# Loading the last y tile of a batched matmul with one DMA of 24 KB runs instead of four of 6 KB runs

## Chip, cores, metric

One core of one Trainium2 chip. The metric is the device time of one execution in microseconds (us). The profiler's span of the same execution is about 1.8 us shorter, and times inside a trace count from the span's start. All runs quoted here are single-core.

## The reference

```python
x: (32, 256, 512) float32      y: (32, 512, 384) float32
out = np.einsum('bij,bjk->bik', x, y).astype(np.float32)      # (32, 256, 384)
```

That is 16.8 MB of x, 25.2 MB of y and 12.6 MB of output.

## The kernel before

The 32 batches go in eight groups of four (n = 0 to 7). For each group x is loaded, rounded to fp16 and transposed on DVE (VectorE); y is loaded and rounded to fp16 on DVE in four casts, each of a quarter of the tile; TensorE multiplies in two halves (e = 0, 1) of 64 matmuls; ACT (ScalarE) and partly DVE copy PSUM to SBUF; the result is stored. All DMAs are issued by SP (SyncE) and so pass through one queue. In the plan below a line is a stage, and each engine keeps the order in which its own parts stand there: x, y and S are a load or a store, T the transposes, R the casts of y, M the matmuls, C the copies on ACT, D those on DVE.

```python
PLAN = """
x0 x1 y0
T0 x2 y1
T1 R0 M0 C0 x3 y2
... (cut)
T5 D3 R4 M4 C4 x7 y6 S2
T6 D4 R5 M5 C5 y7
T7 D5 R6 M6 C6 R7 M7 C7 D7 S3 S4 S5 S6 S7
"""
... (cut: x and y tiles have 2 buffers each, PSUM all 8 banks)
    def load_y(n):
        y_of[n] = y_pool.tile([P, T, K], F32, name="y_sb")       # 128 x 16 x 384 = 24 KB per partition
        src = y[n * Q : (n + 1) * Q].rearrange("g (q t) k -> (g q) t k", t=T)
        step = STEP if n == N - 1 else T                         # STEP = 4: the last y in four pieces
        for a in range(0, T, step):
            keep(nc.sync.dma_start(out=y_of[n][:, a : a + step], in_=src[:, a : a + step]))
...
    def round_y(n):
        y_sb = y_of.pop(n)
        yr_of[n] = yr_pool.tile([P, T, K], MM_DT, name="y_r")
        for a in range(0, T, STEP):                              # four casts
            keep(nc.vector.tensor_copy(yr_of[n][:, a : a + STEP], y_sb[:, a : a + STEP]))
```

In `multiply` the loop over t runs from 0 to 15 with four matmuls each, so the first quarter of a half needs only the first cast of y. Groups 6 and 7 are stored by two DMAs each (S6a, S6b, S7a, S7b), the others by one.

Of the kernel before, what the change touches and what calls it, by code (L numbers as in the profile page):

```python
# [1 line left out]

# [4 lines left out]


MM_DT = mybir.dt.float16
F32 = mybir.dt.float32  # L10
P = 128


Q = 4
STEP = 4
O_BUFS = 5
WIDE_GROUPS = 6
# [8 lines that stand above are left out]
T2 D0 R1 M1 C1 x4 y3 S0  # L26
T3 D1 R2 M2 C2 x5 y4 S1
T4 D2 R3 M3 C3 x6 y5
# [6 lines that stand above are left out]
@with_exitstack  # L35
def kernel(
    ctx: ExitStack,
    tc: tile.TileContext,
    x: bass.AP,
    y: bass.AP,  # L40
    out: bass.AP,
):
    nc = tc.nc

    B, I, J = x.shape
    _, _, K = y.shape

    PQ = P // Q
    R = I // PQ
    T = J // PQ  # L50
    TW = T // 2
    NE = I // P
    N = B // Q

    x_pool = ctx.enter_context(tc.tile_pool(name="x_pool", bufs=2))
    y_pool = ctx.enter_context(tc.tile_pool(name="y_pool", bufs=2))
    xr_pool = ctx.enter_context(tc.tile_pool(name="xr_pool", bufs=1))
    xt_pool = ctx.enter_context(tc.tile_pool(name="xt_pool", bufs=3))
    yr_pool = ctx.enter_context(tc.tile_pool(name="yr_pool", bufs=2))
    o_pool = ctx.enter_context(tc.tile_pool(name="o_pool", bufs=O_BUFS))  # L60
    psum_pool = ctx.enter_context(
        tc.tile_pool(name="psum", bufs=2 * Q, space=bass.MemoryType.PSUM)
    )

    keep = tc.keep_in_program_order




    x_of, y_of, xt_of, yr_of, ps_of, o_of = {}, {}, {}, {}, {}, {}  # L70

    def width(n):
        return PQ if n < WIDE_GROUPS else 2 * PQ

    def on_vector(n, e, g):
        if n < WIDE_GROUPS:
            return (e, g) == (NE - 1, Q - 1)
        return n == N - 1 and g % 2 == 1

    def load_x(n):  # L80
        x_of[n] = x_pool.tile([P, R, J], F32, name="x_sb")
        keep(
            nc.sync.dma_start(  # L83
                out=x_of[n],
                in_=x[n * Q : (n + 1) * Q].rearrange("g (p r) j -> (g p) r j", r=R),
            )
        )

    def load_y(n):
        y_of[n] = y_pool.tile([P, T, K], F32, name="y_sb")  # L90
        src = y[n * Q : (n + 1) * Q].rearrange("g (q t) k -> (g q) t k", t=T)
        step = STEP if n == N - 1 else T
        for a in range(0, T, step):
            keep(nc.sync.dma_start(out=y_of[n][:, a : a + step], in_=src[:, a : a + step]))

    def transpose_x(n):


        x_r = xr_pool.tile([P, R, J], MM_DT, name="x_r")
        keep(nc.vector.tensor_copy(x_r, x_of.pop(n)))  # L100
        xt_of[n] = xt_pool.tile([P, NE, TW, P], F32, name="xt_sb")
        b = width(n) // PQ
        src = x_r.bitcast(F32).rearrange("p (b h e) (q t) -> p b e t h q", b=b, e=NE, t=TW)
        dst = xt_of[n].rearrange("p e t (h s b) -> p b e t h s", s=PQ, b=b)
        for e in range(NE):
            for c in range(b):
                keep(nc.vector.transpose(dst[:, c, e], src[:, c, e]))  # L107
# [4 lines that stand above are left out]
        for a in range(0, T, STEP):  # L112
            keep(nc.vector.tensor_copy(yr_of[n][:, a : a + STEP], y_sb[:, a : a + STEP]))  # L113

    def multiply(n):
        xt = xt_of.pop(n).bitcast(MM_DT).rearrange("p e t (m c) -> p e t m c", c=2)
        y_r = yr_of.pop(n)
        o_of[n] = o_pool.tile([P, R, K], F32, name="o_sb")
        for e in range(NE):
            for g in range(Q):  # L120
                ps_of[n, e, g] = psum_pool.tile([P, K], F32, name="o_ps")
            for t in range(T):
                for g in range(Q):
                    s = slice(g * PQ, (g + 1) * PQ)
                    keep(
                        nc.tensor.matmul(  # L126
                            ps_of[n, e, g],
                            xt[s, e, t // 2, :, t % 2],
                            y_r[s, t],
                            start=(t == 0),  # L130
                            stop=(t == T - 1),
                        )
                    )

    def collect(n, vector):
        w = width(n)
        per = P // w
        copy = nc.vector.tensor_copy if vector else nc.scalar.copy
        o = o_of[n].rearrange("p (u f) k -> p u f k", u=Q // per)
        for e in range(NE):  # L140
            for g in range(Q):
                if on_vector(n, e, g) != vector:
                    continue
                ps = ps_of.pop((n, e, g))
                a = g % per * w
                for h in range(per):
                    keep(copy(o[a : a + w, g // per, h * NE + e], ps[h * w : (h + 1) * w]))  # L147

    def store(n):
        w = width(n)  # L150
        per = P // w
        o = o_of.pop(n).rearrange("p (u f) k -> p u f k", u=Q // per)
        for u in range(Q // per):
            b = n * Q + u * per
            keep(
                nc.sync.dma_start(  # L156
                    out=out[b : b + per].rearrange("g (s f) k -> (g s) f k", s=w),
                    in_=o[:, u],
                )
            )  # L160

    parts = {
        "x": load_x,
        "y": load_y,
        "T": transpose_x,
        "R": round_y,
        "M": multiply,
        "C": lambda n: collect(n, False),
        "D": lambda n: collect(n, True),
        "S": store,  # L170
    }
    for step in PLAN.split():
        parts[step[0]](int(step[1:]))


# [1 line left out]
_INS = ['x', 'y']  # L177
_OUTS = [((32, 256, 384), 'float32')]


# [23 lines left out]
```

## Time and profile before

| | before |
|---|---|
| time, median of the first 3 runs | 135.26 us (134.78 to 135.62) |
| span of the profiled run | 133.3 us |
| bytes moved, mean rate | 54.68 MB, 410 GB/s |
| DMA packets | 4187 |

The rows by engine of the page have one digit per fortieth of the span, 9 being full. The prediction below shows the lines.

### The profile page before, as it was taken

The page shows a single profiled execution, that of the slowest core. Times are in us where ns is not written, and L with a number is a line of the kernel's source. Part 1 is how long each engine was busy: PE and PEld are TensorE (multiplying, and loading weights), DVE is VectorE, ACT ScalarE, POOL GpSimd, SP SyncE. Part 2 cuts the span into 40 slices and gives each one's busy share as a digit, 9 for nine tenths or more (in the row PEclk, how much of TensorE's full clock was granted, in tenths as well). Part 3 has the DMA queues.
Part 4 walks back from the last instruction along what each step waited for, and adds up shares of the span by engine and source line. Part 5 has one row for each costly group of instructions (what it writes and reads, how often), then busy time and mean ns, then how long its engine had stood idle before and what let it go on. Part 6 is the DMA issues. An engine that isn't in the chain of part 4 may idle for free.

```text
span 133.3 us, 2449 instructions
## 1 busy us (share of the span) xinstructions
PE 58.7 (44%) x1024; PEld 35.6 (27%) x1024; DVE 96.3 (72%) x92; ACT 91.5 (69%) x193; POOL 0.2 (0%) x4
## 2 busy tenths in 40 slices
PE   0000004960398039806980079200991398776000
PEld 0000002530255025503450046000560275444000
DVE  0049999699969999999069990999999965255300
ACT  3000000099999999999999997999459999997200
POOL 0000000000000000000000000000000000000000
PEclk9999999998569855995599559955599558999655
DMA  5999999999999999999999999999999999999992
GB/s 103 428 423 438 457 413 423 465 406 423 418 472 428 393 433 430 406 400 449 435 457 392 436 423 452 433 401 452 428 428 389 419 424 443 408 432 425 408 415 107
DMA packets 4187, 54.68 MB, mean 410 GB/s; under 512 B 464, under 2 KB 464, under 8 KB 1488
## 3 DMA queue, kind: packets, MB, share of 16 engines
q1 hardware_dynamic: 4176, 54.53, 97.0%
q8 instruction: 8, 0.13, 0.4%
q14 instruction: 3, 0.02, 0.0%
HBM read 41.94 MB, written 12.58 MB: 409 GB/s over the span
## 4 chain that ended last, share of the span: by engine, by line
DMA 39%; DVE 21%; PE 16%; ACT 15%; issue 1%; DVEq 0%; SPq 0%
DMA x_sb<-in_x_dram 39%; PE o_ps L126 16%; ACT o_sb L147 15%; DVE xt_sb L107 7%; DVE o_sb L147 6%; DVE x_r L100 5%; DVE y_r L113 2%; DVEq L199 0%; SPq L156 0%; DVEq L100 0%; SPq L83 0%
## 5 line engine op out<-in xcount | busy, mean ns | idle before, releaser
L147 ACT COPY o_sb<-o_ps 32x384 f32<-32x384 f32 (+1 forms) x192 | 90.2, 470 | 31.8 <-PE o_ps L126 25.9
L126 PE MATMUL o_ps<-y_r,xt_sb 32*128 32x384 f16 x1024 | 58.7, 389 | 63.5 <-DVE y_r L113 60.7
L126 PEld LDWEIGHTS <-xt_sb 32*128 32x128 f16 x1024 | 35.6, 110 | 86.2 <-issue 54.3
L100 DVE CAST x_r<-x_sb 128x4096 f16<-128x4096 f32 x8 | 18.4, 2294 | 19.0 <-DMA x_sb<-in_x_dram 18.9
L107 DVE STREAM_TRANSPOSE xt_sb<-x_r 128x1024 f32<-128x1024 f32 (+1 forms) x20 | 31.6, 1629 | 0.3
L113 DVE CAST y_r<-y_sb 128x1536 f16<-128x1536 f32 x32 | 28.8, 953 | 3.4 <-DMA y_sb<-in_y_dram 3.2
L147 DVE COPY o_sb<-o_ps 32x384 f32<-32x384 f32 (+1 forms) x32 | 17.8, 556 | 5.4 <-PE o_ps L126 4.9
L147 ACT ACT_TABLE_LOAD x1 | 1.3, 1283 | 0.7 <-PEq L188 0.7
L188 POOL MEMSET const-bfloat16-1.0<- 128x1 bf16 x1 | 0.1, 101 | 0.0
L188 POOL MEMSET const-uint8-127<- 128x1 uint8 x1 | 0.1, 101 | 0.0
L188 POOL MEMSET const-float32-0.0<- 128x1 f32 x1 | 0.1, 98 | 0.2 <-issue 0.2
L188 POOL MEMSET const-float32-1.0<- 128x1 f32 x1 | 0.1, 98 | 0.0
## 6 DMA issues: line engine op xcount, KB each, us to landing
y_sb<-in_y_dram SPq DMA_DIRECT2D x7, 3072.0 KB, 22.9
x_sb<-in_x_dram SPq DMA_DIRECT2D x8, 2048.0 KB, 22.5
out_dram<-o_sb SPq DMA_DIRECT2D x6, 1536.0 KB, 23.0
y_sb<-in_y_dram SPq DMA_DIRECT2D x4, 768.0 KB, 14.8
out_dram<-o_sb SPq DMA_DIRECT2D x4, 768.0 KB, 8.5
```

Of the source, the lines that this page charges most:

```text
L100: keep(nc.vector.tensor_copy(x_r, x_of.pop(n)))
L107: keep(nc.vector.transpose(dst[:, c, e], src[:, c, e]))
L113: keep(nc.vector.tensor_copy(yr_of[n][:, a : a + STEP], y_sb[:, a : a + STEP]))
L126: nc.tensor.matmul(ps_of[n, e, g], xt[s, e, t // 2, :, t % 2], y_r[s, t], start=(t == 0), stop=(t == T - 1),)
L147: keep(copy(o[a : a + w, g // per, h * NE + e], ps[h * w : (h + 1) * w]))
L188: nc = _bacc.Bacc("TRN2", target_bir_lowering=False, num_devices=1)
```

## The change

The last y is treated like the other seven: one DMA whose 128 runs are 24 KB long, in place of four with 128 runs of 6 KB each. A run with a size is a stretch of contiguous bytes in one partition; the page counts a packet for each, and one more for each engine's report that a DMA has ended. The intent is fewer descriptors, completions and issues. What is given up: the first cast could start when a quarter of the tile was there.

```diff
     def load_y(n):
         y_of[n] = y_pool.tile([P, T, K], F32, name="y_sb")
-        src = y[n * Q : (n + 1) * Q].rearrange("g (q t) k -> (g q) t k", t=T)
-        step = STEP if n == N - 1 else T
-        for a in range(0, T, step):
-            keep(nc.sync.dma_start(out=y_of[n][:, a : a + step], in_=src[:, a : a + step]))
+        keep(
+            nc.sync.dma_start(
+                out=y_of[n],
+                in_=y[n * Q : (n + 1) * Q].rearrange("g (q t) k -> (g q) t k", t=T),
+            )
+        )
```

## The prediction

> **What bounds the kernel now.** I read four views in this order: the utilisation in 40 slices, the DMA queue table, the timeline of the last quarter, and the chain of waits. The slices come first because they tell whether anything but the transfers can matter.
>
> ```profile
> DVE  0049999699969999999069990999999965255300
> ACT  3000000099999999999999997999459999997200
> PEclk9999999998569855995599559955599558999655
> DMA  5999999999999999999999999999999999999992
> q1 hardware_dynamic: 4176, 54.53, 97.0%
> HBM read 41.94 MB, written 12.58 MB: 409 GB/s over the span
> ```
>
> The DMA row is at 9 from the second slice to the last but one. One queue carries 54.53 MB and its packets take 97.0% of sixteen engines' whole span. No other row is full to the end: DVE and ACT fall off in slices 33 to 37 while DMA stays at 9. So the 133.3 us are bytes over rate, plus a start and an end of a few us. Compute matters only where it delays a store's issue so far that the queue runs dry.
>
> The timeline of the tail shows the last y at work. Columns: start us, duration us, engine, line, operation, count, and in brackets idle time before it and what ended it.
>
> ```profile
> 104.39 3.56 DVE L113 CAST y_r<-y_sb 128x1536 f16<-128x1536 f32 x4
> 108.40 0.96 DVE L113 CAST y_r<-y_sb 128x1536 f16<-128x1536 f32 x1 [0.45 <-DMA y_sb<-in_y_dram]
> 110.28 0.96 DVE L113 CAST y_r<-y_sb 128x1536 f16<-128x1536 f32 x1 [0.92 <-DMA y_sb<-in_y_dram]
> 112.16 0.96 DVE L113 CAST y_r<-y_sb 128x1536 f16<-128x1536 f32 x1 [0.92 <-DMA y_sb<-in_y_dram]
> 114.01 0.96 DVE L113 CAST y_r<-y_sb 128x1536 f16<-128x1536 f32 x1 [0.89 <-DMA y_sb<-in_y_dram]
> 115.49 2.78 PE L126 MATMUL o_ps<-y_r,xt_sb 32*128 32x384 f16 x63 [0.66 <-ACT o_sb L147]
> 118.23 2.27 DVE L147 COPY o_sb<-o_ps 64x384 f32<-64x384 f32 x4 [3.26 <-PE o_ps L126]
> 119.41 2.75 PE L126 MATMUL o_ps<-y_r,xt_sb 32*128 32x384 f16 x61 [0.66 <-ACT o_sb L147]
> ```
>
> The first row is y6, which one DMA brought: four casts back to back, 3.56 us. The next four are y7, one cast per piece as it lands, 1.85 to 1.88 us apart: 786,432 bytes in 1.88 us is 418 GB/s, the queue's own rate. The two rows of matmuls are the bulk of the two halves of the last multiply (batch group 7). Both waited for **ACT**, which empties PSUM banks of group 6, and not for a cast of y7. The chain of waits says the same: on the pieces leading to 119.41 stand ACT copies, and no y7 cast or load.
>
> **What the Trainium skill says.** (1) "DMA: Bandwidth & Descriptors", section "Anatomy of one DMA — SWDGE (gpsimd) path": a DMA has a fixed cost of about 2 us, mostly the wait until the last byte is confirmed in the target memory. It is stated for another issuing path than this queue's. The trace pays nothing like it per piece when DMAs queue behind each other (pieces 1.88 us apart, all of it bytes). So dropping three DMAs does not drop 6 us.
> (2) The same page, "Why small descriptors are slow (HBM only)": a fixed overhead of about 3 cycles per packet, 27% at 256 bytes. At 6 KB little can be left of it. The trace's packet records agree: median 234 ns for 6,144 bytes and 912 ns for 24,576, that is 26.3 and 26.9 bytes per ns, 2.6% apart.
> (3) "Perfetto Trace Analysis", section "DMA Optimizations": splitting DMAs may let work start sooner when DMA engines are generally idle. Here they are not; the split lets the casts start sooner, but not the transfers.
> (4) DMA page, "Why a DMA increments its semaphore by 16 and not by 1": only the full count means all data has landed, so a cast waits for the slowest of 16 engines. The trace agrees: the completions of y7's last piece spread from 111.77 us over a median of 112.24 to 113.98, and the cast starts at 114.01.
>
> **The change part by part.**
>
> *Transfer.* Removed: four DMAs of 128 packets of 6 KB with 16 completions each; added: one of 128 packets of 24 KB with 16. From the completion records, slowest engine: store S2 ahead of y7 is complete at 106.55 us, the pieces of y7 at 108.38, 110.26, 112.14 and 113.98, so y7 takes 7.43 us. Single-DMA loads of y in the same steady queue took, from the completion ahead to their own, 7.28 (y4), 7.29 (y5) and 7.28 (y6), on the same slowest engine. Saving: **7.43 - 7.28 = 0.15 us** (on the median engine 7.39 against 7.30 to 7.43: nearly nothing). As the queue is full to the end, this saving is on the path, and all stores behind y7 move up by it. y7 then lands at 113.98 - 0.15 = 113.83 us, where its first piece had landed at 108.38.
>
> *Issue.* SP issued the four in 1.75 us from 95.77; one takes 0.33 us. That is some 1.4 us of SP, but the transfer starts only when the queue gets to it, around 106; what follows on SP waits for data much later. Worth 0.
>
> *Casts.* The four casts move from 108.40, 110.28, 112.16 and 114.01 to one row like y6's: start about 113.86, and with 3.56 us for four (0.96 for the first, then 0.87 apart) they end at 114.82, 115.69, 116.55 and 117.42. The last one ended at 114.97 before, so the casts end **2.45 us later**. DVE was idle for 3.26 us in that stretch before its copy at 118.23, so nothing on DVE is pushed, by 0.8 us.
>
> *Matmuls.* Now the casts are read against their readers. Each half of a multiply walks through y in 16 steps of 4 matmuls; a quarter (16 matmuls) uses one cast piece. The first matmuls of the last multiply started before (about 114.3) as banks came free, but the fourth bank came free only at 115.49. From there 63 matmuls take 2.78 us, 44 ns each. The second quarter is wanted at 115.49 + 13 x 0.044 = 116.06, the third at 116.77, the fourth at 117.47. A cast's end reaches PE about 0.14 us later (105.36 to 105.50 in group 6, after the first cast of y6). So the pieces are ready at 114.96, 115.83, 116.69 and 117.56. Late: the last, by 0.09 us. The half ends near 118.36 and not 118.27. The second half stands behind ACT at 118.43 and 119.41, where everything of y7 is long cast: unchanged. **Net on the compute chain: 0.**
>
> *Slack behind that.* Even a real delay would not show at once. The last two stores were issued at about 123.29 and 124.45. The slowest engine reaches them when the store ahead is complete, at 128.60 and 130.44. A transfer in an empty queue needs lead: the first x, issued at 0.73, was complete at 8.48, against 4.89 for its bytes in the steady queue, so some 2.9 us. They were due by 125.7 and 127.5, so 2.4 us of slack in the tighter one, after the 1.1 us (118.3 to 119.4) that PE has in front of its second half.
>
> Sum: -0.15 (transfer) + 0 (issue) + 0 (casts and matmuls) = -0.15 us of 135.26: **135.1 us**.
>
> **The rivals.**
>
> *R1: the lost overlap shows.* Were the last y on the path, the casts' 2.45 us would be added: 137.7 us, slower by 1.8%. For it: y7 is the last load, nothing else hides its casts, and my matmul count leaves only 0.1 us. Against it: both matmul rows waited for ACT, and two slacks (1.1 and 2.4 us) must be used up first. Even if the PE started all of the last multiply after the last cast (117.56 + 2.8 = 120.4, the second half behind it 1 us later than now), the 2.4 us take it.
>
> *R2: fewer, larger descriptors pay.* If each of the three dropped DMAs cost the 2 us of the skill's page in the queue, the time would be 129 us. Against it: the four pieces are spaced at the queue's rate; only 0.15 us over the single loads is there to win.
>
> *R3: chance in the engines.* In the trace two of the 16 engines lag: the slowest minus median completion is 0.4 us early on and 1.74 at y7. y1 took 8.51 us on the slowest where 7.30 is usual. One such hitch more or less is 0.5 to 1.2 us, more than the effect. It sets the width of my range, not its centre.
>
> **Range and chances.** The three runs before span 134.78 to 135.62, that is -0.35% to +0.27%. Taking a little more than that around 135.1 for a new draw gives 134.4 to 135.8. Faster by over 2% (below 132.6) would need 2.7 us out of a full queue whose bytes do not change: 0.5%. Slower by over 2% (above 138.0) needs R1 in full with a hitch as well: 1.5%. Within 2%: 98%.
>
> **What would show each step.** Right: the DMA row stays at 9 to the same slice; packets fall by 3 x 128 + 3 x 16 = 432, from 4187 to 3755; y has eight issues of 3072 KB; the casts of y7 stand as one row of four with 3.56 us, starting near 113.8 after a DVE idle of about 5.9 us; the second half of the last multiply still waits for ACT near 119.4; the last store is issued near 124.4. Wrong: a second-half matmul row waiting for DVE, a last store issued after 127.5, or a dip in the DMA row before the end (R1). If y7's load takes clearly less than 7.2 us, R2 has a part. The prediction fails if engine hitches shift y7 by several us, or if the one large load changes the order in which the queue serves the stores.

## The result, and the profile after

| | before | after |
|---|---|---|
| time, median of 6 runs | 135.2 us (134.78 to 135.62) | 135.1 us (134.89 to 135.37) |
| ratio | 1 | 0.999 (95%: 0.9967 to 1.0013) |
| span of the profiled run | 133.3 us | 133.3 us |
| DMA packets | 4187 | 3755 |

A ratio is the mean time of one kernel's runs over that of the other's of the same rounds, so it is not quite the ratio of the medians. Executions over 1.5% slower than the fastest of the same kernel are left out of the means. The two kernels are the same within 0.3%, and the forecast gain of 0.15 us (0.1%) is smaller than what these runs can tell.

The page of the changed kernel, utilisation in 40 slices, packets, and the y issues (count, size of one, median time to landing):

```profile
DVE  0049999699969999999069990899999940765300
ACT  3000000099999999999999993999959999997200
DMA  5999999989999999999999999999999999999992
DMA packets 3755, 54.68 MB, mean 410 GB/s; under 512 B 416, under 2 KB 416, under 8 KB 928
y_sb<-in_y_dram SPq DMA_DIRECT2D x8, 3072.0 KB, 22.3
```

The DMA row is full up to the same slice as before. DVE has a new hole in the 33rd and 34th slices, where it waits for y7, and nothing follows from it. The timeline of the tail (start us, duration us, engine, line, operation, count, idle time before and what ended it):

```profile
104.62 3.57 DVE L115 CAST y_r<-y_sb 128x1536 f16<-128x1536 f32 x4
111.71 2.76 PE L128 MATMUL o_ps<-y_r,xt_sb 32*128 32x384 f16 x61 [0.57 <-ACT o_sb L149]
114.05 3.57 DVE L115 CAST y_r<-y_sb 128x1536 f16<-128x1536 f32 x4 [5.87 <-DMA y_sb<-in_y_dram]
115.16 3.75 PE L128 MATMUL o_ps<-y_r,xt_sb 32*128 32x384 f16 x67 [0.69 <-DVE y_r L115]
118.60 2.27 DVE L149 COPY o_sb<-o_ps 64x384 f32<-64x384 f32 x4 [0.98 <-ACT o_sb L149]
119.57 2.75 PE L128 MATMUL o_ps<-y_r,xt_sb 32*128 32x384 f16 x61 [0.66 <-ACT o_sb L149]
123.45 1.67 SPq L158 DMA_DIRECT2D out_dram<-o_sb  x2
```

The casts of y7 stand in one row after 5.87 us of idle DVE. The first half of the last multiply now waits for a cast (0.69 us at 115.16) where it had waited for ACT. But the second half starts at 119.57, again after ACT; before it started at 119.41. The last row holds the two stores S7a and S7b: 123.45 and 124.61 us, where they had been at 123.29 and 124.45. This 0.16 us has come down from earlier in the trace: the casts of group 6, which the change does not touch, are at 104.62 instead of 104.39 as well, and ACT's row of copies without a gap, on which the second half waits, begins at 106.83 instead of 106.68.

A trace also records when each of a DMA's 16 engines reports its end. The slowest engine of each, us:

| | before | after |
|---|---|---|
| S2, just ahead of y7 | 106.55 | 106.79 |
| y7, all of it | 113.98 | 114.03 |
| y7 took | 7.43 | 7.24 |
| S5 | 124.94 | 124.98 |
| S7b, the last | 132.26 | 132.30 |

So y7 did get 0.19 us shorter, but this execution came to it 0.24 us later, and both end together. The gain recurs: as one load y7 took 7.23 and 7.21 us in the traces of runs 7 and 8, and in the pair of runs 9 and 10 it took 7.22 us as one load and 7.38 as four.

### The profile page after: what moved, and what is told of

It is laid out like the page before. It is cut to its first block, busy times and chain, and to the rows that moved or that the text cites. A ratio compares the mean times of both kernels' runs of the same rounds, so it can differ in the third digit from the quotient of the medians.

```text
span 133.3 us, 2445 instructions
## 1 busy us (share of the span) xinstructions
PE 60.5 (45%) x1024; PEld 37.4 (28%) x1024; DVE 96.1 (72%) x92; ACT 91.5 (69%) x193; POOL 0.2 (0%) x4
## 2 busy tenths in 40 slices
DMA packets 3755, 54.68 MB, mean 410 GB/s; under 512 B 416, under 2 KB 416, under 8 KB 928
## 4 chain that ended last, share of the span: by engine, by line
DMA 39%; DVE 21%; PE 16%; ACT 14%; issue 1%; DVEq 0%; SPq 0%
DMA x_sb<-in_x_dram 39%; PE o_ps L128 16%; ACT o_sb L149 14%; DVE xt_sb L109 7%; DVE o_sb L149 6%; DVE x_r L102 5%; DVE y_r L115 2%; DVEq L201 0%; SPq L158 0%; DVEq L102 0%; SPq L83 0%
## 5 line engine op out<-in xcount | busy, mean ns | idle before, releaser
L128 PE MATMUL o_ps<-y_r,xt_sb 32*128 32x384 f16 x1024 | 60.5, 396 | 61.8 <-DVE y_r L115 59.8
L128 PEld LDWEIGHTS <-xt_sb 32*128 32x128 f16 x1024 | 37.4, 112 | 84.6 <-issue 52.6
```

Of the source, the lines that this page charges most:

```text
L128: nc.tensor.matmul(ps_of[n, e, g], xt[s, e, t // 2, :, t % 2], y_r[s, t], start=(t == 0), stop=(t == T - 1),)
```

## The experiments

Three questions: what do runs and DMAs cost in a full queue (runs 1 to 3), is the end set by the transfers (run 4), and where did the lost overlap of the casts go (the other six)? `STEP`, `T`, `N` and the plan are those of the code above. Runs 1 to 4 shared one chip and its runs of the kernel before (135.05 us median); the other six were set against runs of it with medians of 135.37 and 135.35 us.

### Run 1, all y loads by one DMA in 6 KB runs

```diff
+        W = RUN * K + 16                    # RUN = 4: 64 bytes of padding after each quarter
-        y_of[n] = y_pool.tile([P, T, K], F32, name="y_sb")
+        y_of[n] = y_pool.tile([P, T // RUN * W], F32, name="y_sb").rearrange("p (a w) -> p a w", w=W)[:, :, : RUN * K]
-                in_=... "g (q t) k -> (g q) t k"
+                in_=... "g (q a r) k -> (g q) a (r k)"
```

(on the changed kernel; the casts read the padded view)

> All eight loads of y go by one DMA each, but in 6 KB runs (the SBUF rows are padded by 64 bytes after each quarter), so the number of DMAs is that of the changed kernel and only the run length differs. Theory (the 0.15 to 0.19 us that y7 gained come from the run length, some 6.5 ns for each of 24 more packets per engine and load): 8 x 24 x 6.5 ns = 1.2 us on a full queue, so about 136.3 us, and each y load takes 7.40 to 7.45 us on the slowest engine. Rival (the gain came from the three DMAs less, their ends and completions): 135.1 us, y loads stay at 7.24 to 7.30 us.

Measured: correct, 135.76 us (135.64 to 135.82), 1.0034 of before (0.9992 to 1.0076). Its page:

```profile
DMA packets 6827, 54.68 MB, mean 408 GB/s; under 512 B 416, under 2 KB 416, under 8 KB 5024
```

The packets rose by 3072 = 8 x 24 x 16 with the same 416 completions, so this changed the run length alone. In the completion records a y load in an undisturbed stretch took 7.42 to 7.45 us on the slowest engine, against 7.28 to 7.30 in the changed kernel: 0.15 us for 24 packets, as the theory had it. (For y7 alone: 7.38 against 7.24.) The total rose by only 0.6 us and not 1.2 (0.44% of 135.1, from the two ratios to the kernel before). Half of the expected total is missing, but the interval of the ratio is wide, some 0.57 us to either side, so that it isn't shown that anything is missing. One place for some of it is in the records: the slowest engine was 1.07 us behind the median one at the end of the changed kernel's trace and 0.75 here, so the median engine ended 0.97 us later and the slowest 0.65.

### Run 2, all y loads by one DMA in 1.5 KB runs

The same edit with `RUN = 1`.

> As the run before, with runs of 1.5 KB: one DMA per y, 2048 packets instead of 128. Theory (a fixed cost of some 6.5 ns per packet): 120 more packets per engine and load, 8 x 120 x 6.5 ns = 6.2 us, about 141.3 us. Rival (only the number of DMAs counts): 135.1 us. If the cost per packet grows as runs get shorter, more than 142.

Measured: correct, 140.84 us (140.79 to 140.89), 1.0413 of before (1.0377 to 1.0449).

```profile
DMA packets 19115, 54.68 MB, mean 393 GB/s; under 512 B 416, under 2 KB 16800, under 8 KB 17312
```

On the slowest engine a y load took 7.9 to 8.2 us (y1 left out, of which more at the end), on average 8.04, 0.75 more than in 24 KB runs: 0.75 / 120 = 6.3 ns for each packet more, and 5.7 / (8 x 120) = 5.9 ns from the total. The rival, that only the number of DMAs counts, is out. The number of packets costs, some 6 ns each, at 6 KB as at 1.5 KB.

### Run 3, all y loads by four DMAs of 6 KB runs

```diff
-        step = STEP if n == N - 1 else T
+        step = STEP
```

(on the kernel before)

> All eight y loads by four DMAs of 6 KB runs each, as the kernel before had it for the last y only. Theory (the queue stays full, only run length costs): the same as one DMA in 6 KB runs, about 136.3 us. Rival A (ends of DMAs cost too): clearly more than that one, up to 8 x 3 x 0.1 us = 2.4 us more. Rival B (the number of DMAs that may be under way limits the prefetch): gaps in the DMA row and over 138 us.

Measured: correct, 136.74 us (136.54 to 136.88), 1.0109 of before (1.0072 to 1.0146).

```profile
DMA  5999999999999999999999999999999999999992
DMA packets 7212, 54.69 MB, mean 406 GB/s; under 512 B 800, under 2 KB 800, under 8 KB 5408
```

This is 0.98 us over run 1 with the same runs and 24 more DMAs, so a DMA more costs about 0.98 / 24 = 0.04 us in the full queue; the records give a little less (four pieces of 1.88 us are 7.52, against 7.44). So I was wrong to put all of the gain down to run length; rival A holds in part. Rival B is out: the DMA row has no gap. Against the changed kernel the total is 1.6 us over eight loads (1.2% of 135.1), 0.2 us per load. That is the change made eight times as large, and it agrees with the 0.19 us that y7 got shorter. How the 0.2 us divide between runs and DMAs stays open within these figures: 0.07 to 0.15 for the runs and 0.08 to 0.12 for the DMAs.

### Run 4, the last y not loaded at all

```diff
     def load_y(n):
+        if n == N - 1:
+            y_of[n] = y_of[n - 1]
+            return
```

(on the changed kernel; wrong in the last four batches)

> Wrong result on purpose in the last four batches: the last y is not loaded, the casts of group 7 read the tile of group 6 again. Theory (bytes over rate sets the end, but the compute chain through ACT stands close behind it): the queue has 7.24 us less to do, but the last store is still issued at about 124.6 and needs some 4.7 us from an empty queue, so the span ends near 130.3 and the time falls by about 3 us to 132. Rival 1 (transfers alone): 7.2 us less, 127.9 us. Rival 2 (the compute chain already sets the end): 135.1 us.

Measured: wrong, 131.9 us (131.25 to 132.25), 0.9746 of before (0.9702 to 0.9791). Its timeline:

```profile
104.55 7.04 DVE L118 CAST y_r<-y_sb 128x1536 f16<-128x1536 f32 x8
119.29 2.76 PE L131 MATMUL o_ps<-y_r,xt_sb 32*128 32x384 f16 x61 [0.66 <-ACT o_sb L152]
123.16 0.33 SPq L161 DMA_DIRECT2D out_dram<-o_sb  x1
```

Now the casts of group 7 are done by 111.6 us, and still the second half starts at 119.29, after ACT, and S7a is issued at 123.16. That shows that y7 never set the pace of the compute chain in the kernel before; ACT did. It also shows the second bound: 7.24 us of transfers less gave 3.2 us.

### Runs 5 and 6, S3, S4 and S5 ahead of the last y

```diff
-T6 D4 R5 M5 C5 y7
-T7 D5 R6 M6 C6 R7 M7 C7 D7 S3 S4 S5 S6 S7
+T6 D4 R5 M5 C5
+T7 D5 R6 M6 C6 S3 S4 S5 y7 R7 M7 C7 D7 S6 S7
```

(run 5 on the changed kernel, run 6 on the kernel before)

> The changed kernel with stores S3, S4 and S5 put ahead of the load of the last y in the queue, so that y7 lands after some 124.8 us instead of 114.0 and no store hides its casts but S6. Theory (the overlap that the split gives is real and was hidden by slack): casts 124.8 to 128.4, last store issued near 134, time about 141.5 us, and 2.4 us slower than its twin with the split load. Rival (the split overlaps nothing of worth, because casts or matmuls hide otherwise): within 0.3 us of the twin.

> The twin: the kernel before (four DMAs for the last y) with S3, S4 and S5 ahead of it. Theory: three of the casts are done when the last piece lands near 125.0, one cast and a quarter of a half multiply follow, last store issued near 131.8, time about 139.3 us, 2.4 us faster than the twin with one load. Rival: the same as the twin within 0.3 us.

Measured: run 5, 146.28 us (144.78 to 147.53; the highest of the four is left out of the ratio), 1.0771 of before; run 6, 142.91 us (142.22 to 143.03), 1.0548. Both correct, both well over what I expected, and 3.4 us apart instead of 2.4. The traces tell why. SP issues in order, and the store S5 had to wait for ACT's copies. In run 5 it was issued at 112.58 us and y7 at 113.01; in run 6 at 111.28 and 111.70. By then little was left in the queue (S4 was complete at 114.18 and 113.75), and y7 was complete only at 129.25 and 127.38 us. The late issue isn't all of it: in run 5 S5 took 5.59 us and y7 9.48, where 3.63 and 7.24 are usual, and why y7 took so long stays open. So the pair mixes two things: a load issued late, by amounts that differ by 1.3 us, and the overlap. From y7's completion to the last store's it took 14.27 us (129.25 to 143.52) and 11.97 (127.38 to 139.35), that is 2.30 us apart, near the 2.4 expected. As times the pair settles nothing; runs 9 and 10 mend it.

### Runs 7 and 8, the casts of the last y twice and three times

```diff
-        for a in range(0, T, STEP):
+        for a in list(range(0, T, STEP)) * (2 if n == N - 1 else 1):      # run 8: 3
```

(on the changed kernel, result unchanged)

> The changed kernel with the four casts of the last y done twice over (same result), so that the last multiply is held back by 3.56 us more. Theory (1.1 us of slack in front of the second half of the last multiply, 2.4 us in front of the last two stores): nearly hidden, 135.1 to 135.5 us, while the last store is issued about 2.4 us later than in the changed kernel. Rival (no slack, the casts of the last y are on the path): 138.7 us.

> The same casts three times over: 7.13 us more. Theory (3.5 us of slack in all, then one for one): 7.1 - 3.5 = 3.6 us slower than the changed kernel, 138.7 us. Rival (no slack): 142.2 us. Second rival (far more slack than I count): 135.1 us.

Measured: twice, 135.43 us (134.87 to 135.66), 0.9992 of before (0.9956 to 1.0029); three times, 138.93 us (138.46 to 139.14), 1.026 (1.0229 to 1.0291). Both correct. Twice, timeline:

```profile
113.99 7.04 DVE L115 CAST y_r<-y_sb 128x1536 f16<-128x1536 f32 x8 [5.87 <-DMA y_sb<-in_y_dram]
118.57 7.93 PE L128 MATMUL o_ps<-y_r,xt_sb 32*128 32x384 f16 x128 [4.46 <-DVE y_r L115]
127.75 1.49 SPq L158 DMA_DIRECT2D out_dram<-o_sb  x2
```

Three times:

```profile
114.34 10.52 DVE L115 CAST y_r<-y_sb 128x1536 f16<-128x1536 f32 x12 [5.84 <-DMA y_sb<-in_y_dram]
122.40 7.49 PE L128 MATMUL o_ps<-y_r,xt_sb 32*128 32x384 f16 x128 [6.88 <-DVE y_r L115]
131.13 1.49 SPq L158 DMA_DIRECT2D out_dram<-o_sb  x2
```

The times came out as the theory had them, yet the stores did not. With the casts twice, S7a is issued 4.3 us later than in the changed kernel (127.75 against 123.45) and not 2.4. The row of matmuls shows why: all 128 take 7.93 us, where the bulk of the two halves had taken 2.78 and 2.75 us in the kernel before (63 and 61 matmuls). In the stretches of the same trace (columns: from:to and length, busy us and count of PE, PEld, DVE, ACT and POOL, granted clock, DMA share, GB/s) the clock is at half:

```profile
118.50:122.50 4.00, 3.93 (x52) 2.23 (x56) 2.53 (x3) 0.66 (x2) 0.00 (x0) 0.50 1.01 427
```

TensorE had stood idle for 4.46 us and started at 0.50 of its clock, 52 matmuls in 4 us or 76 ns each instead of 44. The Trainium skill has this: "TensorE: Matmul & The Clock Gate", section "What's actually happening", gives half rate after an idle window of about 3.4 us and full rate after a busy one. The trace agrees with it here. I had left this out of the sum. In return the queue forgave more than I had counted, and the two errors nearly cancelled.

### Runs 9 and 10, S3 and S4 ahead of the last y

```diff
-T6 D4 R5 M5 C5 y7
-T7 D5 R6 M6 C6 R7 M7 C7 D7 S3 S4 S5 S6 S7
+T6 D4 R5 M5 C5 S3 S4 y7
+T7 D5 R6 M6 C6 R7 M7 C7 D7 S5 S6 S7
```

(run 9 on the changed kernel, run 10 on the kernel before)

> The changed kernel with the stores S3 and S4 ahead of the load of the last y; S5 stays behind it, so that the queue doesn't run low as it did with three. y7 should be complete near 121.4 us. From the run with three stores ahead and one load: the store S7a is issued 9.2 us after that, at 130.6. From the runs with repeated casts: the end moves only by what this exceeds 127.2 us. Theory: 3.4 us later than the changed kernel, about 138.5 us, and 2.1 us slower than the twin with the split load. Rival (the 3.4 us between the first pair came from when the loads were issued and not from the casts' overlap): within 0.5 us of the twin.

> The twin: the kernel before with S3 and S4 ahead of the four loads of the last y. Last piece complete near 121.6 us, store S7a issued 6.8 us later (as in the run with three stores ahead and the split load), at 128.4, which is 1.2 us over what is hidden. Theory: about 136.4 us, 2.1 us faster than the twin with one load. Rival: the same as the twin within 0.5 us.

Measured: one load, 138.67 us (138.53 to 139.68), 1.0247 of before (1.0216 to 1.0278); four loads, 136.31 us (135.47 to 136.59), 1.0061 (1.0019 to 1.0103). Both correct, 2.4 us apart, at the times expected. With one load (this trace is of its slowest run, 139.68 us):

```profile
121.44 3.57 DVE L115 CAST y_r<-y_sb 128x1536 f16<-128x1536 f32 x4 [13.12 <-DMA y_sb<-in_y_dram]
122.55 7.97 PE L128 MATMUL o_ps<-y_r,xt_sb 32*128 32x384 f16 x128 [7.98 <-DVE y_r L115]
131.76 0.33 SPq L158 DMA_DIRECT2D out_dram<-o_sb  x1
```

With four:

```profile
121.73 0.96 DVE L113 CAST y_r<-y_sb 128x1536 f16<-128x1536 f32 x1 [0.91 <-DMA y_sb<-in_y_dram]
122.74 4.14 PE L126 MATMUL o_ps<-y_r,xt_sb 32*128 32x384 f16 x80 [0.40 <-DVE y_r L113]
128.12 1.49 SPq L156 DMA_DIRECT2D out_dram<-o_sb  x2
```

The last bytes of y7 come at nearly the same time (121.42 and 121.71 in the records). With four loads three casts and three quarters of the first half are done by then, and 80 matmuls are left; with one load all 128 are, from a cold clock. The overlap that the split buys is real, but the clock has a part in these two traces: from y7's completion to the issue of S7a they took 10.34 and 6.41 us, 3.9 apart and not 2.4. One stretch of each, one load first:

```profile
122.50:126.50 4.00, 3.95 (x52) 2.30 (x56) 2.51 (x3) 0.00 (x0) 0.00 (x0) 0.50 0.93 390
122.50:126.50 4.00, 3.76 (x76) 2.40 (x79) 2.35 (x5) 1.90 (x4) 0.00 (x0) 0.78 0.96 399
```

The 128 matmuls took 7.97 us here and 6.76 in run 5, where the full clock came back sooner: 1.2 us of clock, about what this run lies above its median (1.0 us). In runs 5 and 6 the two forms were 2.30 us apart. In the case's own plan, with y7 complete at 114, the overlap was hidden.

### The slack, from all of these

| kernel | S7a issued | S7b complete | between |
|---|---|---|---|
| before | 123.29 | 132.26 | 8.97 |
| after | 123.45 | 132.30 | 8.85 |
| casts twice | 127.75 | 132.89 | 5.14 |
| casts three times | 131.13 | 136.28 | 5.15 |
| two stores ahead, one load | 131.76 | 136.91 | 5.15 |
| two stores ahead, four loads | 128.12 | 133.28 | 5.16 |
| three stores ahead, one load | 138.38 | 143.52 | 5.14 |
| three stores ahead, four loads | 134.19 | 139.35 | 5.16 |

In the last six, where S7a sets the end, the end is 5.14 to 5.16 us after its issue (in run 4, not in the table, 5.29: 123.16 to 128.45). In the two kernels it is some 8.9 us after it, because S7a stands in the queue behind other stores. The difference, 8.85 - 5.15 = 3.7 us, is how much later S7a could be issued for nothing. On its own a store of 768 KB is complete 3.26 to 3.31 us after its issue in these six (3.47 in run 4), of which its bytes are 1.83, so its lead is some 1.45 us.

No experiment points to a version that beats both kernels. The best change of order would keep the queue as full as it is.

## Why the prediction was right, point by point

- **The bound.** Right. The DMA row stays full to the same slice; run 4 shows ACT's chain as the second bound, some 3 us behind.
- **Transfer, -0.15 us.** Right in size (y7 took 7.24 us where 7.28 was forecast) and confirmed at eight times its size by run 3. The execution time alone could not have shown it.
- **Issue, 0.** Right, but one of its two reasons was misread: what follows on SP does not wait for data. S3 and S4 had gone out directly after the four loads, at 97.56 and 98.09 us, and now went at 96.38 and 96.90. The other reason holds: the queue comes to S3 only after y7, near 114, so nothing ended sooner.
- **Casts.** Right: one row of 3.57 us after 5.87 us of idle DVE. The start was 114.05 and not 113.86, because the queue came to y7 0.24 us later in this trace.
- **Matmuls.** Right: the second half of the last multiply waits for ACT at 119.57. The first half was held back by more than the 0.09 us forecast: DVE's first copy of its result moved from 118.23 to 118.60, of which 0.16 was there before; the rest, some 0.2 us, was absorbed in front of the second half.
- **Slack.** The conclusion was right; one term was mis-sized. "A transfer in an empty queue needs lead: [...] some 2.9 us" was taken from the very first load of the execution. A late store's lead is 1.45 us, so the stores had 3.7 us of slack and not 2.4. What the step did not count, nor R1's sum of 117.56 + 2.8, is that TensorE restarted at half clock after it had stood idle, which with the casts twice made 128 matmuls take 7.93 us. That runs 7 and 8 still took the times expected is luck: the two errors nearly cancelled. Neither touches the result, in which S7a moved by 0.16 us.
- **R1** is refuted for this plan (runs 4 and 7) and shown to hold once the slack is gone (runs 9 and 10), there with some clock in it. **R2** is refuted: a DMA more costs about 0.04 us here and not 2. **R3**: the spread is there, but part of what I took for chance is not. The load of y1 took 8.3 to 8.7 us on its slowest engine in each of the nine traces in which one DMA of 24 KB runs brings it, and that of y3 7.8 to 8.3.

## What to carry to other kernels

Before you split or merge a transfer in a full queue, find out what its consumer was waiting for: here the last matmuls waited for ACT with either form, and a split that gains 2.4 us where y lands late gains nothing. Merging DMAs of 768 KB saves only some hundredths of a microsecond for each DMA and some 6 ns for each packet of an engine, so it is worth doing when it is free, but the measured time won't show it. Judge slack at the last store's issue: count the bytes still ahead of it in the queue, and remember that TensorE, idle for 4.46 us, restarted at half clock here.

## What the Trainium skill lacked or had wrong

- "DMA: Bandwidth & Descriptors", section "Anatomy of one DMA — SWDGE (gpsimd) path", gives about 2 us fixed per DMA for that path, and no page gives what one more DMA costs on the hardware-issued queue while it is full: about 0.04 us here (24 more DMAs, 0.98 us). On its own a late store of 768 KB had a lead of 1.45 us over its bytes.
- "Why small descriptors are slow (HBM only)", on the same page, has a fixed overhead of about 3 cycles per packet, worked out at 256 bytes; no page gives a time for it in runs of 1.5 to 24 KB. Here it is some 6 ns per packet and engine (24 more packets: 0.15 us per load; 120 more: 0.75 us).
- The same DMA page, section "Where 436 GB/s comes from", says that for transfers between HBM and SBUF the HBM side at about 358 GB/s binds. That doesn't hold for one core alone, which moved 409 GB/s of HBM traffic over the span here, start and end included. The page says so itself in "Measured", just above: 358 is what each core gets when both of a pair stream.
- No page tells that a slow engine's lag may recur at the same load: y1 took 8.3 to 8.7 us on its slowest engine and y3 7.8 to 8.3, where 7.30 is usual, in all nine traces in which they go by one DMA of 24 KB runs. The DMA page, section "Latency and other measured facts", has engines 7 and 15 as usually slower than the others; these records don't number the engines. The cause is open.
